# Seven block products in place of eight in a quarter of a down projection

## The chip, the cores and the metric

The kernel runs on one core of a Trainium2 chip. TensorE multiplies 128x128 blocks and writes into PSUM, VectorE (DVE) and ScalarE (ACT) compute on SBUF and PSUM, GpSimd (POOL) does a little, and SyncE (SP) issues the loads from HBM. The metric is device time in microseconds, from the runs' own clock; the profile shows one execution of the same program, instruction by instruction.

## The reference

One layer of a hybrid trunk on 256 tokens of width 2048, all in float32: a mixer (mLSTM heads, forgetting attention and a gated convolution), then a feed-forward layer, which is what the change touches.

```python
    x = x + jnp.concatenate([y_m, y_a, y_c], axis=-1) @ w_out
    h2 = rmsnorm(x, norm_ffn)
    x = x + jnp.square(jax.nn.relu(h2 @ w_up)) @ w_down
    ...
    return rmsnorm(x, final_norm)
```

`w_up` is 2048x8192 and `w_down` 8192x2048.

## The kernel before

Every large product is made in float32 precision from two rounded parts: an operand is split into a high part (`hi`, type fp32r) and the rest (`lo`), and three products hi*hi, hi*lo and lo*hi are added up in PSUM. Activations are split once; weights are split as they arrive.

The weights come as a stream of units of 1 MiB (`unit`, `load`, L304 and L326), four rows of blocks (k) by 512 columns for `w_down`, into four raw tiles in turn (`NRAW`). A unit is worked in two steps. For step i, ACT copies half a unit to a `hi` tile (L368) and DVE subtracts to get `lo` (L387); there are five tiles of each (`NHL`), so the split of step i+5 can begin only when TensorE is through with step i. When both halves are split, the raw tile is free and SP loads the unit four further on.

The feed-forward layer runs in four quarters of 2048 hidden features. In each, four up blocks (kind "B") give the hidden features transposed, which are joined (L441, L447), squared where positive (L1131) and split into `hid` (L1135, L1137). Then four down blocks (kind "A") of 512 output columns follow one after the other, each over all 16 k of the quarter; a step is 12 matmuls of 512 columns, two k by two halves of the tokens (j) by three products, into two PSUM banks (`mm` and `mx` have four banks each and alternate by block). A finished bank is scaled and added to the residual `x2t` by DVE (L1149).

The order on each engine is not written by hand. A list schedule (`issue`, `best`, `run`, L131 to L171) keeps an estimated clock for each engine, and always issues the task that can start by that clock with the lowest `prio`. The result is a fixed order on each engine, in which the chip then runs the instructions, each with its semaphore waits. DVE's additions to the residual have prio -2, the splits -1, and the two lines that make them are

```python
        a = t_act(ca(1024), hi, deps, prio=prio)
        b = t_dve(cd(1024), lo, [a], prio=prio)
```

Of the kernel before, what the change touches and what calls it, by code (L numbers as in the profile page):

```python
# [33 lines left out]
def trunk(ctx: ExitStack, tc, x, norm_mix, w_in, b_in, mlstm_conv_w, mlstm_conv_b,  # L34
# [24 lines left out]
    # ---- emission: a list schedule on estimated engine clocks  # L59
# [6 lines left out]
    class Buf:  # L66
        """One tile of a rotation of n: taken when the tile n before it has no readers left."""
# [40 lines left out]
    def room(takes):  # L108
        """When the buffers are free; None while a reader of the old tile is not yet issued."""
# [84 lines left out]
    # ---- pools  # L194
# [21 lines left out]
    # ---- loads of x, parameter rows  # L216
# [33 lines left out]
    # x lies where the values and the attention operands come later  # L250
# [6 lines left out]
    # ---- constants  # L257
# [30 lines left out]
    def small(n=2):  # L288
        """Columns of the tile of statistics."""
# [6 lines left out]
    # ---- weight stream  # L296
# [11 lines left out]
    def unit(b, src, c0, k0, last, gates=0, gside=None):  # L308
        """One MiB of weights: columns c0.. of src (and the gate columns beside them)."""
        n = 4 if b.w == 512 else 8  # L310
        units.append(dict(b=b, src=src, c0=c0, ks=list(range(k0, k0 + n)), w=b.w,
                          g=gates, gside=gside, last=last, first=not b.started))
# [43 lines left out]

    def split_tasks(i, deps):
        """High and low parts of half a unit."""
        u, h = divmod(i, 2)
        if u >= len(units):  # L360
            return
        d = units[u]
# [9 lines left out]
        a = t_act(ca(1024), hi, deps, prio=prio)  # L372
# [23 lines left out]

    def matmuls(i, toks):
        u, half = divmod(i, 2)
# [56 lines left out]
    # ---- parameter columns  # L455
# [11 lines left out]
    # the array's clock rises once it is kept busy: transposes of the identity while x arrives  # L467
# [9 lines left out]
    # ---- x: norm, transpose, split  # L477
# [61 lines left out]
    # ---- late constants and parameters  # L539
# [57 lines left out]
    # ---- values  # L597
# [27 lines left out]
    # ---- conformer branch  # L625
# [101 lines left out]
    # ---- the other values, forgetting attention's operands  # L727
# [17 lines left out]
    # ---- gates  # L745
# [14 lines left out]
    def build_gates():  # L760
# [12 lines left out]
        # log1p(e) = ln(u) + (e - (u - 1)) / u with u = fl(1 + e)  # L773
# [503 lines left out]
```

## Time and profile before

| what | us |
|---|---|
| median of 3 runs (1150.33, 1153.60, 1153.37) | 1153.37 |
| the profiled execution, by its span (the page shows no other time of it) | 1148.2 |
| TensorE busy in it | 1133.9 |
| DVE busy | 717.3 |
| ACT busy | 574.3 |

The span runs from the first to the last instruction, so the time of a run is some 5 us longer (1153.37 - 1148.2 = 5.2). Busy time of TensorE counts pipelined matmuls, each from its start to its modelled end, so that one engine can be "99% busy" with matmuls that overlap; what one matmul costs is read from the chain of waits, as a length divided by a count.

### The profile page before, as it was taken

The page shows a single profiled execution, that of the slowest core. Times are in us where ns is not written, and L with a number is a line of the kernel's source. Part 1 is how long each engine was busy: PE and PEld are TensorE (multiplying, and loading weights), DVE is VectorE, ACT ScalarE, POOL GpSimd, SP SyncE. Part 2 cuts the span into 40 slices and gives each one's busy share as a digit, 9 for nine tenths or more (in the row PEclk, how much of TensorE's full clock was granted, in tenths as well). Part 3 has the DMA queues.
Part 4 walks back from the last instruction along what each step waited for, and adds up shares of the span by engine and source line. Part 5 has one row for each costly group of instructions (what it writes and reads, how often), then busy time and mean ns, then how long its engine had stood idle before and what let it go on. Part 6 is the DMA issues. An engine that isn't in the chain of part 4 may idle for free.

```text
span 1148.2 us, 14812 instructions
## 1 busy us (share of the span) xinstructions
PE 1133.9 (99%) x5880; PEld 965.3 (84%) x5880; DVE 717.3 (62%) x978; ACT 574.3 (50%) x807; POOL 17.6 (2%) x40
## 2 busy tenths in 40 slices
PE   8999999999999999999999999999999999999996
PEld 7888888888888888888888888888888888888885
DVE  6679988886665556556545655544655554566553
ACT  6455366777864545444344444333544333454442
POOL 1000000000000000000000000000000000000000
PEclk9999999999999999999999999999999999999999
DMA  8756654557546556655566655566655566655542
GB/s 304 242 184 191 199 164 148 151 153 248 169 162 220 184 185 184 190 199 196 184 189 193 189 193 190 184 191 195 189 193 187 184 192 199 190 189 184 183 147 74
DMA packets 127692, 214.91 MB, mean 187 GB/s; under 512 B 3676, under 2 KB 44936, under 8 KB 127240
## 3 DMA queue, kind: packets, MB, share of 16 engines
q1 hardware_dynamic: 127016, 212.92, 57.9%
q8 instruction: 46, 0.75, 0.3%
q10 hardware_dynamic: 608, 1.06, 0.3%
q14 instruction: 22, 0.18, 0.0%
HBM read 211.87 MB, written 2.10 MB: 186 GB/s over the span
## 4 chain that ended last, share of the span: by engine, by line
PE 97%; DMA 1%; issue 0%; ACT 0%; DVE 0%; SPq 0%; POOL 0%; POOLq 0%; ACTq 0%; DVEq 0%
PE mm L57 64%; PE mx L57 32%; DMA x<-in_x_dram 1%; PE mx L1085 0%; SPq L255 0%; PE mx L846 0%; POOL st L294 0%; PE mx L531 0%; ACT x2t L1188 0%; PE mx L879 0%; DVE lo L387 0%; ACT junk L1175 0%; POOLq L1272 0%; ACT hi L368 0%; PE mx L705 0%
## 5 line engine op out<-in xcount | busy, mean ns | idle before, releaser
L387 DVE TENSOR_TENSOR lo<-raw,hi 128x1024 fp32r<-128x1024 f32 x392 | 480.1, 1225 | 384.8 <-ACT hi L368 383.4
L368 ACT ACTIVATE hi<-raw 128x1024 fp32r<-128x1024 f32 x392 | 415.5, 1061 | 507.4 <-PE mm L57 317.8
L57 PE MATMUL mm<-x,hi 128*128 128x512 f32 x640 | 227.8, 400 | 0.0
L57 PE MATMUL mm<-h,hi 128*128 128x512 f32 x512 | 180.7, 397 | 0.0
L57 PE MATMUL mx<-h,hi 128*128 128x512 f32 x512 | 180.4, 397 | 0.0
L57 PE MATMUL mm<-x,lo 128*128 128x256 f32 x640 | 179.4, 280 | 0.0
L57 PE MATMUL mm<-hi,hid 128*128 128x512 f32 x512 | 159.0, 389 | 0.0
L57 PE MATMUL mx<-hi,hid 128*128 128x512 f32 x512 | 158.9, 389 | 0.0
L57 PEld LDWEIGHTS mm<-x,hi 128*128 128x128 f32 x640 | 120.2, 188 | 28.9 <-ACT tmp L443 0.4
L57 PE MATMUL mm<-h,lo 128*128 128x256 f32 x512 | 143.7, 281 | 0.0
L57 PE MATMUL mx<-h,lo 128*128 128x256 f32 x512 | 143.7, 281 | 0.0
L57 PEld LDWEIGHTS mm<-x,lo 128*128 128x128 f32 x640 | 120.9, 189 | 0.1
L57 PEld LDWEIGHTS mm<-h,hi 128*128 128x128 f32 x512 | 96.1, 188 | 23.3 <-DVE x2t L1073 0.2
L57 PEld LDWEIGHTS mx<-h,hi 128*128 128x128 f32 x512 | 96.1, 188 | 23.3
L57 PEld LDWEIGHTS mm<-hi,hid 128*128 128x128 f32 x512 | 96.1, 188 | 20.1
L57 PEld LDWEIGHTS mx<-hi,hid 128*128 128x128 f32 x512 | 96.1, 188 | 20.0
L57 PE MATMUL mm<-lo,hid 128*128 128x512 f32 x256 | 99.6, 389 | 0.0
L57 PE MATMUL mx<-lo,hid 128*128 128x512 f32 x256 | 99.6, 389 | 0.0
L57 PEld LDWEIGHTS mm<-h,lo 128*128 128x128 f32 x512 | 96.7, 189 | 0.2
L57 PEld LDWEIGHTS mx<-h,lo 128*128 128x128 f32 x512 | 96.7, 189 | 0.0
L57 PE MATMUL mm<-hi,y 128*128 128x512 f32 x256 | 80.4, 392 | 0.0
L57 PE MATMUL mm<-hi,x 128*128 128x512 f32 x192 | 61.6, 396 | 0.0
(191 smaller groups left out, 872.6 us busy)
## 6 DMA issues: line engine op xcount, KB each, us to landing
raw<-in_w_up_dram SPq DMA_DIRECT2D x64, 1024.0 KB, 5.3
raw<-in_w_down_dram SPq DMA_DIRECT2D x64, 1024.0 KB, 5.2
raw<-in_w_in_dram SPq DMA_DIRECT2D x45, 1024.0 KB, 5.3
raw<-in_w_out_dram SPq DMA_DIRECT2D x16, 1024.0 KB, 5.3
raw<-in_w_in_dram SPq DMA_DIRECT2D x4, 1032.0 KB, 5.1
raw<-in_w_in_dram SPq DMA_DIRECT2D x2, 1088.0 KB
x<-in_x_dram SPq DMA_DIRECT2D x8, 256.0 KB, 6.0
x2t<-in_x_dram SPq DMA_DIRECT2D x2, 1024.0 KB
```

The costliest lines, as they stand in the source:

```text
L57: pe.matmul(o, l, r, start=start, stop=stop, skip_group_check=True)
L368: act.activation(t, raws[u][0][:, h * n:(h + 1) * n, :], AF.Copy)
L387: dve.tensor_sub(hl[i][1], raws[u][0][:, h * n:(h + 1) * n, :], hl[i][0].bitcast(F32))
```

## The change

In each quarter the down blocks are taken in pairs (columns 0 to 1023 and 1024 to 2047), and for the second of the four groups of four k (`SV = 1`) the pair's product is made by a method of Strassen's kind: the activations of the group are a 2x2 arrangement of blocks (two k by two halves of the tokens), the weights another (two k by two blocks of 512 columns), and the product takes seven block products of 6 matmuls where it took eight. This is done for seven of the eight pairs; the last pair of the last quarter is left as it was.

For that, the group's activations are summed four ways and split (`x_sums`, once a quarter), and the weights are summed in place in the raw tiles by DVE, four sums a pair (`sum_task`), between the splits. The products run in the order p3, p1, p2, p5, p7, p6, p4 (`SEVEN`). Three go straight into banks of the pair. Four (p1, p5, p6, p7) go into banks of their own, and since the seven products of all quarters are combined in the same way, these four are only accumulated in SBUF (`add_up`): in the first quarter ACT copies them there, in the later ones DVE adds them. In the last quarter that a pair takes part in (quarter 4 for the first pair, 3 for the second) DVE combines the four sums and adds them to the residual: four additions and four scaled additions of 512 columns, with prio -1.5. The load of the last gain (`fnb`, 1 MiB), whose tile now also holds a pair's sums, moves from before the feed-forward layer to the end of that.

```diff
-    def unit(b, src, c0, k0, last, gates=0, gside=None):
-        """One MiB of weights: columns c0.. of src (and the gate columns beside them)."""
+    def unit(b, src, c0, k0, last, gates=0, gside=None, seven=None):
...
+    steps = []
+    sums = {}
+    SEVEN = (("p3", 0, 1), ("p1", 1, 0), ("p2", 1, 1), ("p5", 1, 0), ("p7", 0, 0), ("p6", 0, 1), ("p4", 1, 1))
+    def make_steps():
+        for u, d in enumerate(units):
+            if d["seven"] is None:
+                steps.extend(dict(u=u, h=h, p=None) for h in range(2))
+            elif d["seven"][0]:
+                steps.extend(dict(u=u - 1 + x, h=h, p=p, o=d["seven"][1], e=u) for p, x, h in SEVEN)
+    def piece(u, h):
+        return raws[u][0][:, 2 * h:2 * h + 2, :]
+    def sum_task(i):
+        s = steps[i]
+        e, p = s["e"], s["p"]
+        o, l, r = {"p5": ((e, 0), (e - 1, 0), (e, 0)),
+                   "p7": ((e - 1, 0), (e - 1, 1), (e - 1, 0)),
+                   "p6": ((e - 1, 1), (e - 1, 1), (e, 0)),
+                   "p4": ((e, 1), (e, 1), (e - 1, 1))}[p]
+        after = [halves[i - {"p5": 2, "p7": 3, "p6": 5, "p4": 4}[p]]] + [sums[k] for k in (i - 1, i - 2) if k in sums]
+        sums[i] = t_dve(cd(1024), lambda: dve.tensor_sub(piece(*o), piece(*l), piece(*r)),
+                        after + [loaded[e - 1], loaded[e]], prio=-1)
+        return sums[i]
+    def split_seven(i, deps):
+        s = steps[i]
+        u, h = s["u"], s["h"]
+        if s["p"] in ("p5", "p7", "p6", "p4"):
+            deps = deps + [sum_task(i)]
+        def hi():
+            t = sbt(base, [P, 2, 512], "hi", F32R, bufs=NHL)
+            hl[i] = [t, sbt(base, [P, 2, 512], "lo", F32R, bufs=NHL)]
+            act.activation(t, piece(u, h), AF.Copy)
+        a = his[i] = t_act(ca(1024), hi, deps + [loaded.setdefault(u, Task("none", 0.0, None)), his[i - 1]], prio=-1)
+        halves[i] = t_dve(cd(1024), lambda: dve.tensor_sub(hl[i][1], piece(u, h), hl[i][0].bitcast(F32)),
+                          [a], prio=-1)
+        if s["p"] == "p4":
+            e = s["e"]
+            f1 = [sums[i], halves[i - 1], halves[i - 2]]
+            f2 = [halves[i], halves[i - 3]]
+            c = t_ctl(lambda: load(e - 1 + NRAW, max(t.fin for t in f1)), f1)
+            t_ctl(lambda: load(e + NRAW, max(t.fin for t in f2)), f2 + [c])
+    his = {}
...
+        a = his[i] = t_act(ca(1024), hi, deps + [his.get(i - 1)], prio=prio)
...
+    def seven_matmuls(i):
+        s = steps[i]
+        o, p = s["o"], s["p"]
+        stat = o["hid"]()
+        hi, lo = hl[i]
+        ks = units[s["u"]]["ks"]
+        plain = {"p1": (0, 0), "p2": (2, 0), "p4": (2, 1)}
+        ps = {"p2": lambda: o["b"][0].bufs[0].t, "p3": lambda: o["b"][1].bufs[0].t,
+              "p4": lambda: o["b"][0].bufs[1].t}.get(p, lambda: o["extra"][p].t)()
+        own = p not in ("p2", "p3", "p4")
+        for ii in range(2):
+            if p in plain:
+                m, j = plain[p]
+                k = ks[m + ii] % KC
+                xh = stat[:, k, j * P:(j + 1) * P]
+                xl = stat[:, k, S + j * P:S + (j + 1) * P]
+            else:
+                m = {"p5": 0, "p6": 1, "p7": 2, "p3": 3}[p]
+                xh, xl = (o["sums"]()[:, v_, m, ii, :] for v_ in range(2))
+            mul(ps, xh, hi[:, ii, :], own and ii == 0, False)
+            mul(ps, xh, lo[:, ii, :], False, False)
+            mul(ps, xl, hi[:, ii, :], False, own and ii == 1)
...
-        x2["fn"] = sbt(pl("late"), [P, D], "fnb")
-        nc.sync.dma_start(x2["fn"], bcast(final_norm, D))
...
+    SV = 1
+    xsum, acc = {}, {}
+    def x_sums(q, wb, d, prev):
+        def f1():
+            t = xsum["f"] = sbt(pl("late"), [P, 4, 2, P], "xsum")
+            b11, b21, b12, b22 = (wb.t[:, 2 * k:2 * k + 2, j * P:(j + 1) * P] for k in range(2) for j in range(2))
+            dve.tensor_add(t[:, 0], b21, b22)
+            dve.tensor_sub(t[:, 1], t[:, 0], b11)
+            dve.tensor_sub(t[:, 2], b11, b21)
+            dve.tensor_sub(t[:, 3], b12, t[:, 1])
+        def f2():
+            xsum["s"] = sbt(pl("late"), [P, 2, 4, 2, P], "xsums", F32R)
+            act.activation(xsum["s"][:, 0], xsum["f"], AF.Copy)
+        d = t_dve(4 * cd(256), f1, [d] + prev, prio=-1.85, uses=[wb])
+        a = t_act(ca(1024), f2, [d] + prev, prio=-1.85)
+        return t_dve(cd(1024), lambda: dve.tensor_sub(xsum["s"][:, 1], xsum["f"], xsum["s"][:, 0].bitcast(F32)),
+                     [a], prio=-1.85)
+    def fn_in():
+        x2["fn"] = sbt(pl("late"), [P, D], "fnb")
+        nc.sync.dma_start(x2["fn"], bcast(final_norm, D))
+    def add_up(p, q, o, fin):
+        ts = []
+        for m, x in enumerate(("p1", "p5", "p6", "p7")):
+            def f(m=m, x=x):
+                if (p, 0) not in acc:
+                    acc[p, 0] = sbt(pl("late"), [P, 4, 512], "acc0") if p == 0 else \
+                        sbt(pl("late"), [P, D], "fnb").rearrange("p (m n) -> p m n", m=4)
+                t = acc[p, 0][:, m, :]
+                if q == 0:
+                    act.activation(t, o["extra"][x].t, AF.Copy)
+                else:
+                    dve.tensor_add(t, t, o["extra"][x].t)
+            deps = [o["done"][x], late_open] + ts[-1:]
+            if q == 0:
+                ts.append(t_act(ca(512, True), f, deps, prio=-2, uses=[o["extra"][x]]))
+            else:
+                ts.append(t_dve(cd(512), f, deps, prio=-2, uses=[o["extra"][x]]))
+        if not fin:
+            return []
+        def g(i):
+            a1, a5, a6, a7 = (acc[p, 0][:, m, :] for m in range(4))
+            def out(j, c, t):
+                dve.scalar_tensor_tensor(x2[0][:, j, cut(c)], t, rs2[:, j:j + 1], x2[0][:, j, cut(c)],
+                                         op0=OP.mult, op1=OP.add)
+            if i == 0:
+                dve.tensor_add(a6, a6, a1)
+                out(0, 2 * p, a1)
+            elif i == 1:
+                dve.tensor_add(a7, a7, a6)
+                out(1, 2 * p, a7)
+            elif i == 2:
+                dve.tensor_add(a6, a6, a5)
+                out(0, 2 * p + 1, a6)
+            else:
+                dve.tensor_add(a5, a5, a7)
+                out(1, 2 * p + 1, a5)
+        gs = [ts[-1]]
+        for i in range(4):
+            gs.append(t_dve(2 * cd(512), lambda i=i: g(i), [gs[-1], rs_t], prio=-1.5))
+        return gs[1:]
...
+        t0, t1 = (("mm", "mx"), ("mx", "mm"))[q % 2]
         for c in range(4):
-            b = block_units(blk("B", 512, lambda: big["h"], "h", tag()), w_up, 2048 * q + 512 * c)
+            b = block_units(blk("B", 512, lambda: big["h"], "h", (t0, t1)[c % 2]), w_up, 2048 * q + 512 * c)
...
+            if c == SV:
+                chunk["sums%d" % q] = x_sums(q, wb, done_zz, prev)
         hid_readers = []
+        def down(c, tg):
+            return blk("A", 512, lambda: big["hid"], "hid%d" % q, tg)
+        bs, shared = {}, {}
+        for p in range(2):
+            if q == 3 and p == 1:
+                for c in (2, 3):
+                    bs[c] = block_units(down(c, t1), w_down, 512 * c, KC * q)
+                continue
+            b0, b1 = bs[2 * p], bs[2 * p + 1] = down(2 * p, t0), down(2 * p + 1, t0)
+            names = ("p1", "p5", "p6", "p7")
+            o = dict(b=(b0, b1), tag=t1, hid=lambda: big["hid"], sums=lambda: xsum["s"], q=q,
+                     extra={x: Buf(mx_rot if t1 == "mx" else mm_rot) for x in names},
+                     done={x: Task("pe", 0.0, None) for x in names})
+            for g in range(4):
+                k0 = KC * q + 4 * g
+                if g == SV:
+                    unit(b1, w_down, 1024 * p + 512, k0, False, seven=(0, o))
+                    unit(b0, w_down, 1024 * p, k0, False, seven=(1, o))
+                else:
+                    unit(b0, w_down, 1024 * p, k0, g == 3)
+                    unit(b1, w_down, 1024 * p + 512, k0, g == 3)
+            got = add_up(p, q, o, q == (3, 2)[p])
+            for i, t in enumerate(got):
+                shared[2 * p + i // 2, i % 2] = t
+            if p == 1 and got:
+                fn_t = t_ctl(fn_in, got)
         for c in range(4):
-            b = block_units(blk("A", 512, lambda: big["hid"], "hid%d" % q, tag()), w_down, 512 * c, KC * q)
+            b = bs[c]
...
+            p, o = steps[i]["p"], steps[i]["o"]
+            new = [o["extra"][p]] if p in o["extra"] else []
+            need = [halves[i], chunk["sums%d" % o["q"]]] + [chunk[d["b"].key, k % KC] for k in d["ks"]]
+            force(lambda: all(t.fin is not None for t in need) and room(new) is not None)
+            start = max([clock["pe"], room(new)] + [t.fin + LAT for t in need])
+            take(new)
+            for x_ in new:
+                x_.t = bank(o["tag"])
+            seven_matmuls(i)
+            clock["pe"] = start + 1.3
+            if new:
+                o["done"][p].fin = clock["pe"]
+            split_tasks(i + NHL, [done_at(clock["pe"])])
+            extras()
+            continue
```

The first place where the order matters is DVE in the second quarter, where the down products begin. Before, its rows are these (`lo` is a weight split, `zz` and `hid` the hidden features, `x2t` the residual):

```order
L447 TENSOR_TENSOR z<-tmp,mx 128x256 x4
L1131 SCALAR_TENSOR_TENSOR zz<-z 128x1024
L387 TENSOR_TENSOR lo<-raw,hi 128x1024 x2
L1137 TENSOR_TENSOR hid<-zz,hid 128x4x256
L387 TENSOR_TENSOR lo<-raw,hi 128x1024 x6
L1149 SCALAR_TENSOR_TENSOR x2t<-mm,st,x2t 128x512 x2
L387 TENSOR_TENSOR lo<-raw,hi 128x1024 x8
L1149 SCALAR_TENSOR_TENSOR x2t<-mx,st,x2t 128x512 x2
```

With the change, DVE's rows there, from the split of the fourth product on (line numbers are those of the changed kernel; L383 sums raw weights, L399 splits the weights of a product, L1218 adds a product in the bank `mm` to `acc0`, L443 splits the weights of ordinary steps, and a bracket names the engines whose semaphores a row waits for):

```order
L399 TENSOR_TENSOR lo_6250<-raw_6096,hi_6249 128x1024 [waits Activation_49]
L399 TENSOR_TENSOR lo_6260<-raw_6057,hi_6259 128x1024 [waits Activation_49]
L1218 TENSOR_TENSOR acc0_4918<-acc0_4918,mm_6262 128x512 [waits PE_49]
L399 TENSOR_TENSOR lo_6271<-raw_6057,hi_6270 128x1024 [waits Activation_49]
L1218 TENSOR_TENSOR acc0_4918<-acc0_4918,mm_6280 128x512 [waits PE_49]
L383 TENSOR_TENSOR raw_6096<-raw_6096,raw_6057 128x1024
L1218 TENSOR_TENSOR acc0_4918<-acc0_4918,mm_6298 128x512 [waits PE_49]
L1218 TENSOR_TENSOR acc0_4918<-acc0_4918,mm_6289 128x512
L399 TENSOR_TENSOR lo_6306<-raw_6096,hi_6305 128x1024 [waits Activation_49]
L443 TENSOR_TENSOR lo_6313<-raw_6138,hi_6312 128x1024 [waits DMAHW7_49,Activation_49]
```

Between the splits there now stand the additions of p1, p5, p6 and p7, in this order, each after a product of TensorE. The split of the seventh product (`lo_6306`, of p4) comes behind the last two of them. The same order stands in quarters 3 and 4 for the first pair.

In the fourth quarter the first pair's sums are also combined. DVE's rows from the sum for p4 on:

```order
L383 TENSOR_TENSOR raw_8826<-raw_8826,raw_8787 128x1024
L1218 TENSOR_TENSOR acc0_4918<-acc0_4918,mm_9028 128x512 [waits PE_49]
L1218 TENSOR_TENSOR acc0_4918<-acc0_4918,mm_9019 128x512
L1236 TENSOR_TENSOR acc0_4918<-acc0_4918 128x512 [waits DVE_49]
L1232 SCALAR_TENSOR_TENSOR x2t_2582<-acc0_4918,st_99,x2t_2582 128x512
L1239 TENSOR_TENSOR acc0_4918<-acc0_4918 128x512 [waits DVE_49]
L1232 SCALAR_TENSOR_TENSOR x2t_2582<-acc0_4918,st_99,x2t_2582 128x512 [waits DVE_49]
L1242 TENSOR_TENSOR acc0_4918<-acc0_4918 128x512
L1232 SCALAR_TENSOR_TENSOR x2t_2582<-acc0_4918,st_99,x2t_2582 128x512 [waits DVE_49]
L1245 TENSOR_TENSOR acc0_4918<-acc0_4918 128x512
L1232 SCALAR_TENSOR_TENSOR x2t_2582<-acc0_4918,st_99,x2t_2582 128x512 [waits DVE_49]
L399 TENSOR_TENSOR lo_9036<-raw_8826,hi_9035 128x1024 [waits Activation_49]
```

The eight rows of L1236 to L1245 and L1232 moved in ahead of the seventh product's split (`lo_9036`).

The third place is DVE for the second pair of the third quarter, where that pair's sums are combined; the rows from the split of the first ordinary step on (`lo_7952`):

```order
L443 TENSOR_TENSOR lo_7952<-raw_7813,hi_7951 128x1024 [waits DMAHW7_49,Activation_49]
L1218 TENSOR_TENSOR fnb_5218<-fnb_5218,mx_7968 128x512 [waits PE_49]
L1218 TENSOR_TENSOR fnb_5218<-fnb_5218,mx_7954 128x512
L1236 TENSOR_TENSOR fnb_5218<-fnb_5218 128x512 [waits DVE_49]
L1232 SCALAR_TENSOR_TENSOR x2t_2582<-fnb_5218,st_99,x2t_2582 128x512
L1239 TENSOR_TENSOR fnb_5218<-fnb_5218 128x512 [waits DVE_49]
L1232 SCALAR_TENSOR_TENSOR x2t_2582<-fnb_5218,st_99,x2t_2582 128x512 [waits DVE_49]
L1242 TENSOR_TENSOR fnb_5218<-fnb_5218 128x512
L1232 SCALAR_TENSOR_TENSOR x2t_2582<-fnb_5218,st_99,x2t_2582 128x512 [waits DVE_49]
L1245 TENSOR_TENSOR fnb_5218<-fnb_5218 128x512
L1232 SCALAR_TENSOR_TENSOR x2t_2582<-fnb_5218,st_99,x2t_2582 128x512 [waits DVE_49]
L443 TENSOR_TENSOR lo_7965<-raw_7813,hi_7964 128x1024 [waits Activation_49]
```

Here the seventh product's split is already ahead, and what stands behind the additions and the combination is the split of the second ordinary step (`lo_7965`).

## Rows read from the trace of the kernel before

**Rows 1.** The page: the span, the engines' busy times, and TensorE's granted clock by 40 slices

```profile
span 1148.2 us, 14812 instructions
PE 1133.9 (99%) x5880; PEld 965.3 (84%) x5880; DVE 717.3 (62%) x978; ACT 574.3 (50%) x807; POOL 17.6 (2%) x40
...
PEclk9999999999999999999999999999999999999999
```

**Rows 2.** The chain of waits in order of time: start, length, engine and line of two blocks

```profile
1029.38 22.61 PE mx L57 x128
...
1073.77 21.76 PE mx L57 x96
```

**Rows 3.** Busy time of the engines in the down products of the third quarter

```profile
874.48:961.54 87.06, 87.06 (x385) 72.07 (x385) 46.70 (x44) 35.21 (x35) 0.00 (x0) 1.00 0.59 193
```

**Rows 4.** Groups of instructions by line, the whole span

```profile
L387 DVE TENSOR_TENSOR lo<-raw,hi 128x1024 fp32r<-128x1024 f32 x392 | 480.1, 1225 | 384.8 <-ACT hi L368 383.4
L368 ACT ACTIVATE hi<-raw 128x1024 fp32r<-128x1024 f32 x392 | 415.5, 1061 | 507.4 <-PE mm L57 317.8 <-PE mx L57 182.5 <-issue 2.9
...
L664 DVE SCALAR_TENSOR_TENSOR cacc<-ypad,colp,cacc 128x256 f32<-128x256 f32 x120 | 51.7, 479 | 0.0
...
L1131 DVE SCALAR_TENSOR_TENSOR zz<-z 128x1024 f32<-128x1024 f32 x16 | 19.6, 1225 | 0.5
...
L1149 DVE SCALAR_TENSOR_TENSOR x2t<-mm,st,x2t 128x512 f32<-128x512 f32 x16 | 11.2, 745 | 0.0
...
L1073 DVE TENSOR_TENSOR x2t<-x2t,mm 128x512 f32<-128x512 f32 x8 | 5.1, 680 | 0.0
L1066 ACT ACTIVATE junk<-x2t 128x512 bf16<-128x512 f32 x8 | 5.0, 622 | 0.1
...
L1157 DVE TENSOR_TENSOR x2t<-x2t,fnb 128x512 f32<-128x512 f32 x6 | 3.9, 686 | 0.0
```

**Rows 5.** The timeline where the first down product begins, ACT and DVE

```profile
519.77 1.05 ACT L368 ACTIVATE hi<-raw 128x1024 fp32r<-128x1024 f32 x1
520.36 1.23 DVE L1131 SCALAR_TENSOR_TENSOR zz<-z 128x1024 f32<-128x1024 f32 x1
522.25 1.06 ACT L368 ACTIVATE hi<-raw 128x1024 fp32r<-128x1024 f32 x1 [1.43 <-PE mm L57]
523.22 1.04 ACT L1135 ACTIVATE hid<-zz 128x1024 fp32r<-128x1024 f32 x1
```

**Rows 6.** The timeline 11 us later, at a step's end

```profile
529.98 0.62 PE L57 MATMUL mm<-hi,hid 128*128 128x512 f32 x2
530.41 1.06 ACT L368 ACTIVATE hi<-raw 128x1024 fp32r<-128x1024 f32 x1 [1.66 <-PE mm L57]
...
531.50 1.23 DVE L387 TENSOR_TENSOR lo<-raw,hi 128x1024 fp32r<-128x1024 f32 x1 [1.49 <-ACT hi L368]
```

**Rows 7.** Issues of the weight loads: size and time to landing

```profile
raw<-in_w_down_dram SPq DMA_DIRECT2D x64, 1024.0 KB, 5.2
```

**Rows 8.** The timeline of TensorE near the start of the span

```profile
8.56 0.23 PE L461 MATMUL mx<-ident,rowp 16*128 16x16 f32 x1
12.38 3.36 PE L531 MATMUL mx<-ident,x 128*128 128x128 f32 x16 [3.60 <-DVE x L511]
```

**Rows 9.** Busy time and granted clock by stretches, start and end of the span

```profile
10.00:12.00 2.00, 0.00 (x0) 0.00 (x0) 1.10 (x5) 1.90 (x4) 0.01 (x1) 1.00 1.05 407
12.00:14.00 2.00, 1.61 (x9) 1.62 (x10) 1.93 (x5) 1.17 (x3) 2.00 (x5) 0.69 1.06 402
14.00:16.00 2.00, 2.00 (x10) 1.63 (x8) 1.10 (x2) 2.00 (x5) 0.01 (x1) 0.50 1.04 382
16.00:18.00 2.00, 1.86 (x7) 1.14 (x7) 2.00 (x4) 2.00 (x4) 0.00 (x0) 0.96 1.06 389
...
1139.00:1140.00 1.00, 0.05 (x1) 0.00 (x0) 0.88 (x2) 0.40 (x2) 0.00 (x0) 1.00 1.05 346
...
1142.00:1143.00 1.00, 0.00 (x0) 0.00 (x0) 0.88 (x2) 0.72 (x1) 0.00 (x0) 0.78 0.00 0
```

More of the change, by code (lines that the diff above doesn't have):

```diff
@@ L306, in __init__ @@
             self.need = {}
-    def unit(b, src, c0, k0, last, gates=0, gside=None):
+    def unit(b, src, c0, k0, last, gates=0, gside=None, seven=None):
         n = 4 if b.w == 512 else 8
         units.append(dict(b=b, src=src, c0=c0, ks=list(range(k0, k0 + n)), w=b.w,
-                          g=gates, gside=gside, last=last, first=not b.started))
+                          g=gates, gside=gside, last=last, first=not b.started, seven=seven))
         b.started = True
@@ L357, in split_tasks @@
+    his = {}
     def split_tasks(i, deps):
-        u, h = divmod(i, 2)
-        if u >= len(units):
+        if i >= len(steps):
             return
+        if steps[i]["p"]:
+            split_seven(i, deps)
+            return
+        u, h = steps[i]["u"], steps[i]["h"]
         d = units[u]
@@ L371, in split_tasks @@
         prio = -1 if i >= NHL else -2.005 + 0.02 * i
-        a = t_act(ca(1024), hi, deps, prio=prio)
+        a = his[i] = t_act(ca(1024), hi, deps + [his.get(i - 1)], prio=prio)
         last = [a]
@@ L395, in split_tasks @@
             t_ctl(lambda: load(u + NRAW, max(t.fin for t in frees)), frees)
+    def seven_matmuls(i):
[20 more added lines that the diff above has]
+            mul(ps, xl, hi[:, ii, :], False, own and ii == 1)
     def matmuls(i, toks):
-        u, half = divmod(i, 2)
+        u, half = steps[i]["u"], steps[i]["h"]
         d = units[u]
@@ L1102, in trunk @@
     z_rot, zz_rot = Rot(2), Rot(2)
-    flip = [0]
-    def tag():
-        flip[0] ^= 1
-        return ("mx", "mm")[flip[0]]
+    SV = 1
[15 more added lines that the diff above has]
+                     [a], prio=-1.85)
@@ L1114, in trunk @@
     for q in range(4):
-        down_of = []
+        t0, t1 = (("mm", "mx"), ("mx", "mm"))[q % 2]
         for c in range(4):
-            b = block_units(blk("B", 512, lambda: big["h"], "h", tag()), w_up, 2048 * q + 512 * c)
+            b = block_units(blk("B", 512, lambda: big["h"], "h", (t0, t1)[c % 2]), w_up, 2048 * q + 512 * c)
             zb, wb = Buf(z_rot), Buf(zz_rot)
@@ L1131, in f1 @@
                 dve.scalar_tensor_tensor(wb.t, zb.t, 0.0, zb.t, op0=OP.max, op1=OP.mult)
-            d = t_dve(cd(1024), f1, js[1:], prio=-1.9, takes=[wb], uses=[zb])
+            d = done_zz = t_dve(cd(1024), f1, js[1:], prio=-1.9, takes=[wb], uses=[zb])
             prev = hid_readers if q else []
@@ L1154, in trunk @@
                         junk[:, 0:512], x2[0][:, j, cut(c)], AF.Square, scale=D ** -0.5,
-                        accum_out=ss3[:, 4 * j + c:4 * j + c + 1]), [d], prio=-2)
+                        accum_out=ss3[:, 4 * j + c:4 * j + c + 1]), [d, shared.get((c, j))], prio=-2)
                     fsq[j].append(a)
                     fin_t[j].append(t_dve(cd(512), lambda j=j, c=c: dve.tensor_mul(
-                        x2[0][:, j, cut(c)], x2[0][:, j, cut(c)], x2["fn"][:, cut(c)]), [a], prio=-1))
+                        x2[0][:, j, cut(c)], x2[0][:, j, cut(c)], x2["fn"][:, cut(c)]), [a, fn_t], prio=-1))
+    make_steps()
     last = units[-1]["b"]
@@ L1197, in trunk @@
     NU = len(units)
-    items = [(i, (0, 1)) for i in range(2 * NU - 4)]
+    NS = len(steps)
+    items = [(i, (0, 1)) for i in range(NS - 4)]
     for j in range(2):
-        items += [(i, (j,)) for i in range(2 * NU - 4, 2 * NU)]
+        items += [(i, (j,)) for i in range(NS - 4, NS)]
     dma[0] = 7.9
@@ L1208, in trunk @@
     for i, toks in items:
-        u, half = divmod(i, 2)
+        u, half = steps[i]["u"], steps[i]["h"]
         d = units[u]
+        if steps[i]["p"]:
+            p, o = steps[i]["p"], steps[i]["o"]
[13 more added lines that the diff above has]
+            continue
         b = d["b"]
```

## The prediction, made before the changed kernel was run

> **What bounds the kernel now.** Read the page first: TensorE is busy for 1133.9 of 1148.2 us, DVE for 717.3, ACT for 574.3, and the granted clock is at full speed in all 40 slices [rows 1]. Busy time could mislead, so the chain of waits comes next: in the feed-forward layer it is TensorE alone, block after block, an up block 22.61 us and a down block 21.76 us for 96 matmuls [rows 2]. One matmul of the down product thus costs 21.76 / 96 = 0.227 us, an ordinary step of 12 costs 2.72, one of 6 costs 1.36. Nothing in that chain is a wait. So a matmul less is time gained, as long as its operands come in time; the rest of this text is about whether they do. In the timeline ACT's copy starts some 0.2 us after the next step has begun (530.21 is the second start in the first row), having sat idle 1.66 us for TensorE; DVE's split follows at once after 1.49 us idle [rows 6]. In the down product DVE is busy 46.70 of 87.06 us [rows 3]. The cover is there, but it is 1.5 us a step and not one long stretch.
>
> **What the change removes.** Six matmuls in each of 7 pairs: 42 x 0.227 = 9.5 us, all on the path. [...]
>
> **What it adds, by pair.** Three more copies at 1.061 us on ACT; on DVE three more splits and four sums in place, seven at 1.225 (the split has the same shape), and from the second quarter on four additions from PSUM at 0.68 [rows 4]. That is 8.6 + 2.7 = 11.3 us of DVE for a pair, 22.6 in a quarter. With the 46.7 of [rows 3] it makes 69.3 us of 84.3, so as an average DVE still has room. The sums of the activations (four additions of 256 columns, at most 0.479 each, and one copy and split, 3.2 us of DVE) lie in the up product a whole block ahead of their use, beside idle time; I cost them at nothing. The load of the gain goes between two weight loads, behind DVE's last combination; the load queued behind it needs a later split on DVE anyway, lands 5.2 us after its issue [rows 7] and is read seven steps (19 us) later: nothing. Up to the first of these sums the order of all engines is that of before, but for the gain's load. PSUM: a pair takes the four banks of one kind, and a bank is emptied by 0.745 us of DVE while another block's two steps (5.4 us) run: nothing.
>
> **Where the order bites.** Count from the first matmul of the seven products; they end at 1.36, 2.72, ... and the seventh (p4) should start at 8.16 and wants its `lo` for its second matmul, at 8.39. A result can be read 0.2 us after its grid time.
>
> *First pair, quarters 2, 3 and 4.* DVE's order has the addition of p6 ahead of the split for p4. p6 is the sixth product, ready at 8.16 + 0.2 = 8.36, after which come two additions (1.36) and the split (1.225): 10.95, and 11.0 at TensorE with a hand-over of 0.05. TensorE wanted it at 8.39, so it stands 2.6 us. It doesn't win this back, since it is the bound. The next split is ready 1.2 us later, when the seventh product still runs and the next one wants it 1.36 us on: no second stall. In quarter 4 the combination stands ahead of that split too: four additions at 0.686 [rows 4] and four scaled additions. For the latter no row has 512 columns from SBUF; between 0.479 (256 columns) and 1.225 (1024) a straight line gives 0.73. Together 5.7, so 2.6 + 5.7 = 8.3 us.
>
> *Second pair, quarter 3.* The seventh split is in time, and so is the first ordinary one (done at 8.8). Behind it: two additions to 10.1, the combination to 15.8, then the second ordinary split, 17.0. TensorE wants that at 12.24 + 0.23 = 12.47: 4.6 us.
>
> *Quarter 1.* ACT does the copying, and the copy for the seventh product stands behind that of p5, which is ready at 5.64: 5.64 + 0.62 + 1.06 + 1.225 = 8.6: 0.2 us late for the first pair; for the second pair everything is in time, as it is in quarter 2 (p5's addition done at 6.3, the seventh split at 7.5).
>
> Stalls: 0.2 + 2.6 + 2.6 + 8.3 + 4.6 = 18.3 us. Against 9.5 saved: 8.8 us longer.
>
> **Does a waiting instruction hold those behind it?** That carries the sum. The trace shows it on ACT: `zz` was done at 521.59, yet the copy of `hid` from it waited until 523.22, behind a copy of weights for which ACT sat idle 1.43 us [rows 5]. No row shows it of DVE, where it could be worth anything from nothing to 18 us; I take it to be as on ACT, which is built into the program in the same way. [...]
>
> **The clock.** Near the start TensorE stood 3.6 us [rows 8]. [...] The stalls of 8.3 and 4.6 us are longer than the gap at the start, those of 2.6 shorter. I charge the two long ones half of 3.4 us each, 3.4 together, bounded below by nothing and above by 6.8 (all four).
>
> **Sum.** 1148.2 - 9.5 + 18.3 + 3.4 = 1160.4 us of span. The median of the runs is 5.2 us above this execution's span, which lies outside it: 1165.6 us, 1.1% slower. Bounds: without a clock effect 1162; with it at all four stalls 1169; scaled additions at 0.48 instead of 0.73 take 2 us off, at 1.225 they would add 4.
>
> **Rivals.**
> *The additions don't hold the splits* (DVE passes over a waiting addition, or finds p6 ready). Decisive point: the split for p4 done by 8.39. Then all is hidden but 0.2 us, and the time is 1153.4 - 9.5 + 0.2 = 1144, faster. For it: the averages of [rows 3], 15 us of idle DVE in a quarter even after the change. Against: the rows of the order, and ACT's held copy. Chance 0.07.
> *Only the waits hold, not the combinations*: if the eight combination rows took far less time or TensorE ran on during them, the stalls would be 0.2 + 3 x 2.6 = 8.0, with no long gap for the clock: 1153.4 - 9.5 + 8.0 = 1151.9, no change. Against: the additions of 512 columns have a row. Chance 0.07.
> *DVE becomes the bound after the stalls.* In the 9.5 us of a seven-product run it has 11 x 1.225 + 2.7 = 16.2 us of work; if the lead of five steps is used up before, each of the next steps waits as well, 1 to 2 us a pair, and the clock falls more often: above 1171. For it: that figure. Against: in the up product and the first four steps it has 1.5 us free a step [rows 6]. Chance 0.1.
>
> **How the numbers follow.** The forecast has 0.76 and its own range is 1159 to 1171. To hold 8 in 10 the range reaches a little toward the second rival: 1157 to 1171. A measurement of this kernel can tell about 0.3% (3.5 us) from no change: faster below 1149.9, slower above 1156.8. The forecast, the third rival and a sliver of the second are slower: 0.87; no change 0.06; faster 0.07.
>
> **What would show it.** TensorE: 5838 matmuls in place of 5880; a gap of some 2.6 us before the second matmul of the seventh product in the first pair of quarters 2 and 3, 8 us in quarter 4, 4.6 us in the second pair of quarter 3 before the second ordinary step, each with DVE's split as the releaser; DVE idle 0.8 us before the addition of p6. A granted clock of 0.5 after the two longest. Right but for the clock: gaps as said and full clock. Wrong: no gap above 1 us in the down products, or gaps at every step.

## The result, and the profile after

The changed kernel takes **1166.3 us** (median of 4 runs, 1164.51 to 1167.03) against 1152.01 for the kernel before (4 runs, 1150.33 to 1153.6): a ratio of 1.0123, 95% interval 1.0106 to 1.0141. It is slower by 1.2%; the prediction was 1165.6.

The page of the changed kernel, with the span and the engines as in [rows 1]; the profiled execution took 1167.01 us. Of the clock's 40 slices the first and the 38th show 8 tenths, where all showed 9 before:

```profile
span 1164.9 us, 14898 instructions
PE 1135.5 (97%) x5838; PEld 962.3 (83%) x5838; DVE 804.3 (69%) x1083; ACT 602.3 (52%) x840; POOL 17.6 (2%) x40
```

The 42 matmuls are gone (5838 for 5880), yet TensorE shows 1.6 us more busy time: a matmul at half clock is shown longer (0.63 us for 0.39), and the up blocks of quarter one took longer too (last section). What TensorE waited for, over the whole span (total, times, longest):

```profile
PE mx L57 <- DVE lo L399: 8.7, 2, 7.1
PE mm L57 <- DVE lo L443: 3.8, 1, 3.8
...
PE mm L57 <- DVE lo L399: 1.6, 1, 1.6
...
PE mx L57 <- ACT hi L396: 0.7, 2, 0.4
PE mm L57 <- ACT hi L396: 0.4, 1, 0.4
```

L399 is the split of the low part for the seven products, L443 that for ordinary steps, L396 the copy of the high part for the seven products; `...` stands for waits at the start of the span. The seven waits lie in four places: 0.4 for `hi` and then 1.6 for `lo` in the first pair of quarters two and three, 3.8 in quarter three's second pair, 0.4 and 7.1 in quarter four. All are waits for DVE's split or for the copy ahead of it, where [rows 2] had none. The longest, in the timeline of DVE and then of TensorE:

```profile
1078.59 1.28 DVE L1218 TENSOR_TENSOR acc<-acc,mm 128x512 f32<-128x512 f32 x2 [0.90 <-PE mm L57]
1079.79 0.69 DVE L1236 TENSOR_TENSOR acc<-acc 128x512 f32<-128x512 f32 x1
...
1084.55 0.75 DVE L1232 SCALAR_TENSOR_TENSOR x2t<-acc,st,x2t 128x512 f32<-128x512 f32 x1
1085.22 1.22 DVE L399 TENSOR_TENSOR lo<-raw,hi 128x1024 fp32r<-128x1024 f32 x1
```

```profile
1078.92 0.50 PE L57 MATMUL mx<-hi,hid 128*128 128x512 f32 x1 [0.37 <-ACT hi L396]
1086.50 0.79 PE L57 MATMUL mx<-lo,hid 128*128 128x512 f32 x1 [7.07 <-DVE lo L399]
```

DVE stands idle 0.90 us for the sixth product, adds two products, does the eight rows of the combination, and only then the split that TensorE has wanted since 1079.15, one matmul start after 1078.92.

The down products of the four quarters, the last to the end of the span: length, then the busy time of PE, PEld, DVE, ACT and POOL, the granted clock, DMA's share and GB/s. Before, they were 87.06 [rows 3], and 1148.2 - 1051.99 = 96.2 for the last [rows 1, 2]:

```profile
522.45:607.04 84.59, 84.59 (x373) 69.75 (x373) 62.31 (x58) 44.77 (x49) 0.00 (x0) 1.00 0.58 199
697.48:786.00 88.52, 86.51 (x373) 70.89 (x373) 66.93 (x66) 40.99 (x41) 0.00 (x0) 0.98 0.55 190
876.44:969.04 92.60, 86.79 (x373) 70.87 (x373) 72.15 (x74) 41.01 (x41) 0.00 (x0) 0.98 0.56 193
1059.49:1164.90 105.41, 88.71 (x378) 72.29 (x377) 66.13 (x80) 42.74 (x58) 1.87 (x2) 0.93 0.38 130
```

Quarter one gains 2.5 us; the others lose 1.5, 5.5 and 9.2. That is +13.7 of the +16.7 us between the two spans; the other 3.0 lie outside the change (last section). The granted clock by short stretches, after the waits of quarters two, three (second pair) and four:

```profile
720.00:723.00 3.00, 3.00 (x8) 2.32 (x7) 3.00 (x4) 1.71 (x2) 0.00 (x0) 0.50 0.95 309
...
948.00:952.00 4.00, 3.67 (x9) 2.96 (x10) 4.00 (x5) 0.00 (x0) 0.00 (x0) 0.57 0.85 317
...
1082.00:1091.00 9.00, 4.50 (x11) 3.54 (x12) 8.93 (x11) 1.72 (x2) 0.00 (x0) 0.50 0.37 132
```

With the slices beside them these are 3.4, 3.4 and 10.2 us at half clock (granted 0.50). There a matmul starts 0.42 us after the one ahead (949.78 and 950.20) in place of 0.227, so by these two starts about half of such a stretch is lost, as far as TensorE works in it.

### The profile page after: what moved, and what is told of

It reads as the page before. It is cut to its first block, busy times and chain, and to the rows that moved or that the text cites. A ratio compares the mean times of both kernels' runs of the same rounds, so it can differ in the third digit from the quotient of the medians.

```text
span 1164.9 us, 14898 instructions
## 1 busy us (share of the span) xinstructions
PE 1135.5 (97%) x5838; PEld 962.3 (83%) x5838; DVE 804.3 (69%) x1083; ACT 602.3 (52%) x840; POOL 17.6 (2%) x40
## 3 DMA queue, kind: packets, MB, share of 16 engines
q10 hardware_dynamic: 608, 1.06, 0.3%
## 4 chain that ended last, share of the span: by engine, by line
PE 95%; DVE 2%; DMA 1%; issue 1%; ACT 0%; POOL 0%; POOLq 0%; ACTq 0%; DVEq 0%
PE mm L57 65%; PE mx L57 29%; DMA x<-in_x_dram 1%; DVE lo L399 0%; DVE x2t L1232 0%; DVE lo L443 0%; PE mx L1162 0%; DMA rowp<-in_norm_mix_dram 0%; DVE acc L1218 0%; PE mx L925 0%; POOL st L294 0%; PE mx L610 0%; ACT x2t L1362 0%; PE mx L958 0%; DVE fnb L1218 0%
## 5 line engine op out<-in xcount | busy, mean ns | idle before, releaser
L443 DVE TENSOR_TENSOR lo<-raw,hi 128x1024 fp32r<-128x1024 f32 x364 | 442.5, 1224 | 288.4 <-ACT hi L424 287.0
L424 ACT ACTIVATE hi<-raw 128x1024 fp32r<-128x1024 f32 x364 | 384.2, 1061 | 426.9 <-PE mm L57 282.1
L57 PE MATMUL mm<-x,hi 128*128 128x512 f32 x640 | 227.8, 400 | 0.0
L57 PE MATMUL mm<-h,hi 128*128 128x512 f32 x512 | 181.5, 399 | 0.0
L57 PE MATMUL mx<-h,hi 128*128 128x512 f32 x512 | 181.2, 399 | 0.0
L57 PE MATMUL mm<-x,lo 128*128 128x256 f32 x640 | 179.5, 280 | 0.0
L57 PE MATMUL mm<-hi,hid 128*128 128x512 f32 x556 | 174.6, 391 | 0.4 <-ACT hi L396 0.4
L57 PEld LDWEIGHTS mm<-x,hi 128*128 128x128 f32 x640 | 120.2, 188 | 28.8 <-ACT tmp L522 0.4
L57 PE MATMUL mm<-h,lo 128*128 128x256 f32 x512 | 143.8, 281 | 0.0
L57 PE MATMUL mx<-h,lo 128*128 128x256 f32 x512 | 143.8, 281 | 0.0
L57 PEld LDWEIGHTS mm<-hi,hid 128*128 128x128 f32 x556 | 105.2, 189 | 22.7 <-ACT hi L396 0.8
L57 PEld LDWEIGHTS mm<-x,lo 128*128 128x128 f32 x640 | 120.9, 189 | 0.1
L57 PEld LDWEIGHTS mm<-h,hi 128*128 128x128 f32 x512 | 96.2, 188 | 24.0 <-DVE x2t L1150 0.2
L57 PEld LDWEIGHTS mx<-h,hi 128*128 128x128 f32 x512 | 96.2, 188 | 23.9
L57 PE MATMUL mm<-lo,hid 128*128 128x512 f32 x278 | 109.3, 393 | 5.4 <-DVE lo L443 3.8
L57 PE MATMUL mx<-hi,hid 128*128 128x512 f32 x328 | 106.0, 399 | 0.7 <-ACT hi L396 0.7
L57 PEld LDWEIGHTS mm<-h,lo 128*128 128x128 f32 x512 | 96.7, 189 | 0.1
L57 PEld LDWEIGHTS mx<-h,lo 128*128 128x128 f32 x512 | 96.7, 189 | 0.1
L396 ACT ACTIVATE hi<-raw 128x1024 fp32r<-128x1024 f32 x49 | 52.1, 1064 | 66.2 <-DVE raw L383 27.0
L57 PE MATMUL mm<-hi,y 128*128 128x512 f32 x256 | 80.4, 392 | 0.0
L57 PEld LDWEIGHTS mx<-hi,hid 128*128 128x128 f32 x328 | 63.4, 193 | 15.2 <-ACT hi L396 1.6
L57 PE MATMUL mx<-lo,hid 128*128 128x512 f32 x164 | 65.8, 401 | 8.7 <-DVE lo L399 8.7
```

What stands on the lines that cost most here:

```text
L57: pe.matmul(o, l, r, start=start, stop=stop, skip_group_check=True)
L396: act.activation(t, piece(u, h), AF.Copy)
L424: act.activation(t, raws[u][0][:, h * n:(h + 1) * n, :], AF.Copy)
L443: dve.tensor_sub(hl[i][1], raws[u][0][:, h * n:(h + 1) * n, :], hl[i][0].bitcast(F32))
```

## The experiments

The theory under test: what costs is work that stands ahead of a split in DVE's order, plus the clock behind each wait, and not the amount of DVE's work. Its rivals: DVE has too much to do in whatever order, or the clock falls for reasons of its own.

### The splits first

Three priorities of the program's list schedule, so that a split which is ready goes ahead:

```diff
-                ts.append(t_act(ca(512, True), f, deps, prio=-2, uses=[o["extra"][x]]))
+                ts.append(t_act(ca(512, True), f, deps, prio=-0.9, uses=[o["extra"][x]]))
...
-                ts.append(t_dve(cd(512), f, deps, prio=-2, uses=[o["extra"][x]]))
+                ts.append(t_dve(cd(512), f, deps, prio=-0.9, uses=[o["extra"][x]]))
...
-            gs.append(t_dve(2 * cd(512), lambda i=i: g(i), [gs[-1], rs_t], prio=-1.5))
+            gs.append(t_dve(2 * cd(512), lambda i=i: g(i), [gs[-1], rs_t], prio=-0.8))
```

> The changed kernel, with the accumulations (lines 1222 and 1224) and the combinations (line 1250) given a later priority than the splits; every instruction stays, the matmuls too, so the saved 42 x 0.227 = 9.5 us stay as well. Only two additions of a pair, of its first and fourth products, can still stand ahead of the seventh product's split.
> Theory (what costs is work that stands ahead of a split on DVE, in order, and the clock that falls behind it): the waits for lo L399 (8.7 + 1.6 us) and for lo L443 (3.8 us) go, and so do the stretches at half clock behind them (about 7 us, from the quarters' lengths: 2.5 in each of three). 1166.3 - 14 - 7 = about 1145, range 1141 to 1149, ratio to before 0.991 to 0.997, with the granted clock at 1.00 through all four down quarters.
> Rival 1 (DVE has too much to do in the eleven steps of a group, in whatever order): the waits come back at later splits or at the next up block, 1158 or more.
> Rival 2 (the clock falls for a reason of its own, not behind waits): the waits go and the half clock stays, about 1152.

Measured: **1142.57 us** (5 runs, 1141.25 to 1144.2), ratio to before **0.9921** (0.9909 to 0.9933). The page (span 1142.1 us), all that TensorE still waited for, DVE's timeline at the place in quarter two where the changed kernel had its wait, and the four down products:

```profile
PE 1128.1 (99%) x5838; PEld 958.7 (84%) x5838; DVE 803.9 (70%) x1083; ACT 601.3 (53%) x840; POOL 17.6 (2%) x40
```

```profile
PE mx L610 <- DVE x L590: 3.0, 1, 3.0
PE mm L550 <- POOL gb L272: 1.4, 1, 1.4
PE mm L57 <- ACT x L594: 0.2, 1, 0.2
```

```profile
712.42 1.22 DVE L383 TENSOR_TENSOR raw<-raw 128x1024 f32<-128x1024 f32 x1
713.55 1.28 DVE L1218 TENSOR_TENSOR acc<-acc,mm 128x512 f32<-128x512 f32 x2
714.84 1.22 DVE L399 TENSOR_TENSOR lo<-raw,hi 128x1024 fp32r<-128x1024 f32 x1
715.99 5.76 DVE L443 TENSOR_TENSOR lo<-raw,hi 128x1024 fp32r<-128x1024 f32 x5
721.90 1.23 DVE L443 TENSOR_TENSOR lo<-raw,hi 128x1024 fp32r<-128x1024 f32 x1 [0.15 <-ACT hi L424]
723.04 0.68 DVE L1218 TENSOR_TENSOR acc<-acc,mm 128x512 f32<-128x512 f32 x1
```

```profile
522.56:607.17 84.61, 84.61 (x374) 69.76 (x373) 62.23 (x58) 44.70 (x49) 0.00 (x0) 1.00 0.58 199
697.62:781.96 84.34, 84.34 (x373) 69.84 (x373) 66.92 (x66) 40.94 (x41) 0.00 (x0) 1.00 0.58 200
872.40:956.75 84.35, 84.35 (x374) 69.85 (x373) 72.16 (x74) 40.95 (x41) 0.00 (x0) 1.00 0.60 205
1047.19:1142.10 94.91, 85.70 (x378) 70.62 (x377) 65.77 (x80) 42.68 (x58) 1.87 (x2) 0.97 0.42 144
```

The same instructions in another order, with the same DVE work in quarter two (66.92 and 66.93 us), and every wait behind the span's start is gone, and in the down products the half clock too (1.00 in the first three; the 0.97 of the last goes to the end of the span, and up to 1127.0 it is 1.00 as well). Both rivals fall. Only two additions, of the first and the fourth product, still stand ahead of the seventh split, and DVE waits for neither; the third comes only after six ordinary splits, when DVE has idle time again, and the fourth after one more. Quarters two and three are now 87.06 - 84.35 = 2.7 us shorter than before, which is the twelve matmuls saved in a quarter at 0.227. This version beats both kernels.

### The combinations alone held back

```diff
-            gs.append(t_dve(2 * cd(512), lambda i=i: g(i), [gs[-1], rs_t], prio=-1.5))
+            gs.append(t_dve(2 * cd(512), lambda i=i: g(i), [gs[-1], rs_t, o["done"]["sum"]], prio=-1.5))
...
+    def release(i):
+        for i7, o in after_seven:
+            for x in o["late"]:
+                if i == i7 + o["late"][x]:
+                    o["done"][x].fin = clock["pe"]
...
```

> The changed kernel, with the combinations alone (line 1250) held until five ordinary steps behind the seventh product; the four accumulations of a pair stay where they are.
> Theory (each piece of work ahead of a split is charged by itself): the wait of the first pair in quarter four falls from 7.1 us to that of quarters two and three (1.6 us for lo L399), the wait of quarter three's second pair (3.8 us) goes; three equal waits of some 2 us in all are left. 1166.3 - 5.5 - 3.8 = 1157.0 by the waits alone, and up to 5 us less if the clock no longer falls at those two places: 1152 to 1157, most likely 1154, ratio 1.002 to 1.005.
> Rival (the accumulations alone hold the split, the combination is taken up by slack behind it): no change, about 1166.

Measured: 1150.52 us (12 runs), ratio 0.9998 (0.9989 to 1.0007). The down products of quarters two to four:

```profile
695.83:782.75 86.92, 84.90 (x373) 69.75 (x373) 66.85 (x66) 40.92 (x41) 0.00 (x0) 1.00 0.58 194
873.19:960.12 86.93, 84.91 (x374) 69.75 (x373) 69.91 (x72) 40.94 (x41) 0.00 (x0) 1.00 0.54 184
1050.56:1148.00 97.44, 86.26 (x378) 70.53 (x377) 65.60 (x80) 42.68 (x58) 1.87 (x2) 0.98 0.41 140
```

Against the splits-first version each is longer by 2.58, 2.58 and 2.53 us. That is the price of a pair's accumulations where the changed kernel has them, without a combination and the same in three places. That it comes out level with before was not expected: my range began at 1152, because I left some of the half clock in place, and here it fell at none of the three waits (1.00 from 714 to 724, 891 to 901 and 1069 to 1079 us). The rival (1166) is far off: against the first profile of the changed kernel quarter three is 5.7 us shorter and quarter four 8.0, which is what the combinations cost there, with their waits and what the clock took behind them.

### A ladder of waits

Accumulations and combinations held back, and the seventh split written several times:

```diff
-        halves[i] = t_dve(cd(1024), lambda: dve.tensor_sub(hl[i][1], piece(u, h), hl[i][0].bitcast(F32)),
+        halves[i] = t_dve(cd(1024), lambda: [dve.tensor_sub(hl[i][1], piece(u, h), hl[i][0].bitcast(F32)) for _ in range(1 + (s["o"]["again"] if s["p"] == "p4" else 0))],
...
+            o = dict(again=(2, 3, 3, 5, 4, 4, 1)[2 * q + p], b=(b0, b1), tag=t1, hid=lambda: big["hid"], sums=lambda: xsum["s"], q=q,
...
```

> The changed kernel with accumulations and combinations held until two to five steps behind the seventh product, so that none stands ahead of a split, and with the seventh product's split (line 399) written again 2, 3, 3, 5, 4, 4 and 1 times in the seven pairs in their order (each 1.22 us on DVE, the same values again). This makes seven waits of TensorE of seven sizes: by the recurrence of the steps about 2.2, 1.6, 3.4, 4.0, 4.7, 2.8 and 1.0 us.
> Theory 1 (the clock falls behind a wait above some size): waits up to 1.6 us leave the clock at 1.00, those from 2.8 us on are each followed by a stretch at 0.50, and each costs the time of a stall plus about 2 to 2.5 us; 19.7 us of waits, 8 to 13 us of clock, so a span of about 1170 to 1178.
> Theory 2 (whether the clock falls does not go by the wait's size): some of the waits from 2.8 us on leave the clock at 1.00, or one below 1.7 us drops it.

One run, 1167.58 us with a span of 1165.5. The seven waits in TensorE's timeline, in order:

```profile
540.61 0.50 PE L57 MATMUL mm<-lo,hid 128*128 128x512 f32 x1 [1.73 <-DVE lo L399]
...
584.49 0.50 PE L57 MATMUL mm<-lo,hid 128*128 128x512 f32 x1 [1.43 <-DVE lo L399]
...
720.44 0.79 PE L57 MATMUL mx<-lo,hid 128*128 128x512 f32 x1 [2.99 <-DVE lo L399]
...
769.63 0.50 PE L57 MATMUL mx<-lo,hid 128*128 128x512 f32 x1 [3.94 <-DVE lo L399]
...
908.40 0.79 PE L57 MATMUL mm<-lo,hid 128*128 128x512 f32 x1 [4.25 <-DVE lo L399]
...
956.25 0.50 PE L57 MATMUL mm<-lo,hid 128*128 128x512 f32 x1 [2.69 <-DVE lo L399]
...
1089.64 0.50 PE L57 MATMUL mx<-lo,hid 128*128 128x512 f32 x1 [0.47 <-DVE lo L399]
```

In the first pairs one, two, three and four extra splits give 0.47, 1.73, 2.99 and 4.25 us: 1.26 more for each; in the second pairs three, four and five give 1.43, 2.69 and 3.94. Once the slack is gone, one instruction more ahead of the split costs TensorE the time by which DVE starts the next row later. That is 1.26 us here, where the copies write the same tile (five of them span 6.26 us from 902.09 on); the five splits of different tiles in the splits-first version span 5.76, which is 1.14 for each. This is the order's effect measured by itself, with no wait of DVE for TensorE in it. The clock behind the third, fourth, fifth and sixth of them:

```profile
720.00:726.00 6.00, 5.56 (x13) 4.40 (x14) 6.00 (x6) 1.06 (x1) 0.00 (x0) 0.50 0.74 254
...
771.00:774.00 3.00, 3.00 (x9) 2.35 (x8) 3.00 (x3) 1.06 (x1) 0.00 (x0) 0.50 0.92 335
...
908.00:914.00 6.00, 5.60 (x13) 4.44 (x14) 6.00 (x6) 1.06 (x1) 0.00 (x0) 0.50 0.75 241
...
952.00:962.00 10.00, 7.31 (x32) 5.74 (x32) 9.90 (x10) 4.25 (x4) 0.00 (x0) 1.00 0.69 231
```

With the slices beside them, 6.8 us at half clock at the wait of 2.99 and again at that of 4.25, but 3.4 at that of 3.94 and none at that of 2.69: what the clock takes does not grow with the wait. In this one run it fell behind the three longest waits and none of the shorter ones, as theory 1 has it; against theory 1 stands the first profile of the changed kernel, where it fell behind a wait of 1.64. The span came out below the 1170 to 1178 that were expected: by the lengths of the down products the waits cost about 19 us (19.7 expected) and the clock 7.6 (8 to 13), and the rest of this execution is 3.0 us shorter than in the splits-first profile (its first down product starts at 519.57, there at 522.56).

### The changed kernel twice more

> The changed kernel once more, unchanged, for a second profile. In its first profile the equal waits of quarters two and three (0.38 and 1.64 us) left the clock at 1.00 in one place and dropped it in the other, and the waits of 3.8 and 7.1 us dropped it both times.
> Theory (which waits drop the clock does not go by their size alone, and differs between executions): the waits stand at the same places with the same sizes to 0.1 us, the stretches at half clock at others or of other lengths; the span moves by 1 to 3 us with them.
> Rival (the program fixes it): the same three stretches, after the first wait of quarter two, after quarter three's second pair and in quarter four, and the up blocks of quarter one at 22.61 us again.

> The same once more, a third profile of the changed kernel: if the stretches at half clock are fixed by the program, all three profiles agree in their places and lengths; if not, at least one of the three differs, most likely at one of the two short waits (0.4 and 1.6 us) of the first pairs of quarters two and three.

1162.49 and 1166.05 us, spans 1160.3 and 1164.0, both on another chip than the experiments above. The seven waits stand in the same places and agree to 0.01 us in all three profiles. The clock does not. The second profile is 4.6 us shorter than the first, more than the 1 to 3 that were expected, but 3.1 of that lie ahead of the first down product. Its down products of quarters two to four, with full clock in quarter two:

```profile
694.40:781.31 86.91, 84.90 (x374) 69.76 (x373) 66.84 (x66) 40.93 (x41) 0.00 (x0) 1.00 0.57 194
871.75:964.39 92.64, 86.83 (x374) 70.80 (x373) 72.17 (x74) 40.92 (x41) 0.00 (x0) 0.98 0.56 193
1054.83:1160.30 105.47, 88.90 (x379) 72.44 (x377) 66.13 (x80) 42.65 (x58) 1.87 (x2) 0.93 0.39 130
```

and the third profile's clock at the four places:

```profile
718.00:721.00 3.00, 3.00 (x9) 2.35 (x8) 3.00 (x4) 1.22 (x2) 0.00 (x0) 0.50 0.96 341
...
896.00:898.00 2.00, 2.00 (x6) 1.52 (x6) 2.00 (x3) 1.14 (x2) 0.00 (x0) 0.50 0.97 242
...
947.00:953.00 6.00, 5.69 (x13) 4.46 (x14) 4.80 (x5) 0.59 (x1) 0.00 (x0) 0.50 0.80 282
...
1083.00:1089.00 6.00, 2.33 (x6) 1.87 (x7) 5.93 (x8) 0.00 (x0) 0.00 (x0) 0.50 0.12 33
```

At the first pair's wait of quarters two and three the clock fell once in the first profile, never in the second, both times in the third. So the waits are the same in all three executions, and the clock behind them differs from one to the next; the second and the third profile come from the same chip. Why it differs was not tried.

## Why the prediction was right

**The saving.** 42 matmuls at 0.227 were to give 9.5 us. The splits-first version shows them: its down products are 2.5, 2.7, 2.7 and 1.3 us shorter than before, 9.2 in all, with 0.25 in quarter one lost to the copy on ACT that was priced at 0.2 (that order on ACT is the same in the splits-first version).

**The order of DVE.** The step that carried the sum, that a waiting instruction on DVE holds those behind it, was inferred from ACT's rows. Now there are rows of DVE itself, in quarter two of the changed kernel:

```profile
713.86 0.69 DVE L1218 TENSOR_TENSOR acc<-acc,mm 128x512 f32<-128x512 f32 x1 [0.89 <-PE mm L57]
714.47 1.22 DVE L383 TENSOR_TENSOR raw<-raw 128x1024 f32<-128x1024 f32 x1
...
715.80 1.06 ACT L396 ACTIVATE hi<-raw 128x1024 fp32r<-128x1024 f32 x1 [4.63 <-DVE raw L383]
```

DVE sits idle 0.89 us for the fourth product (p5), and behind that addition stands the sum for the seventh (L383), which waits for no engine. It starts 16.99 us after the quarter's first down product (714.47 - 697.48). In the splits-first version it starts after 14.80 (712.42 - 697.62), when p5 has only begun; so it could have run, and was held. The sign that was named, DVE idle 0.8 us ahead of the sixth product's addition, came true as well (0.89 in this quarter, 0.90 in quarter four), but shows less: the split behind it got its `hi` only at 716.86 (715.80 + 1.06), after that idle time, which ended at 716.58.

The prediction left this hold out: the sum and the `hi` copy of the seventh product are nowhere on its path, and the wait of 0.4 for `hi` was not foreseen. The size came out right because the path that was foreseen ends last: the split could begin at 716.86, and the additions of p6 and p7 keep it until 717.78. By these rows about 1.6 of the 2.6 us would stay if those two additions alone were moved; that is an estimate, which no run tried.

**The stalls**, each as the length of a down product over the splits-first version's, with the half clock behind it taken off:

- First pair, quarters two and three, predicted 2.6: the second profile has 86.91 - 84.34 = 2.57, at full clock.
- Second pair, quarter three, predicted 4.6: 92.64 - 84.35 - 2.57 = 5.7, of which half of 3.4 is clock: 4.0.
- Quarter four, predicted 8.3: 105.47 - 94.91 = 10.6, of which half of the 5.6 us at half clock after the wait's end is clock: 7.8.

With 0.25 they sum to 17.2 against 18.3. The combination was mis-sized: its scaled addition takes 0.75 for the estimated 0.73, but the eight rows run from 1079.79 to 1085.22, 5.4 and not 5.7, since here a row of DVE begins a little before the one ahead has run its shown length (the two additions ahead, 1.28 us long from 1078.59, end at 1079.87).

**The clock.** This step was the weakest. I charged 3.4 us: half of 3.4 at each of the two long waits. The 3.4 is an estimate from [rows 9]: between 1.00 and 0.50, the shares of the clock from 12 to 18 us make (0.62 + 1 + 0.08) x 2 us at half clock after the gap at the start. No run shows 3.4 for the two long waits together; it was 1.7 + 2.6 = 4.3 and 1.7 + 2.8 = 4.5 in the first two profiles. In the first profile the clock took about 1.7 in quarter two (where I had charged nothing), 1.7 in quarter three and 2.6 in quarter four: 6.0, inside the bounds of 0 to 6.8. In the second it took 1.7 and 2.8, together 4.5, and in the third 7.6 by the lengths of the down products (88.55, 95.25 and 104.34 us), above the bounds. The argument by a wait's length alone failed: 2.0 us of idle time dropped the clock in some executions, 2.69 in the ladder did not.

**The sum.** The span was forecast at 1160.4; the three profiles have 1160.3, 1164.0 and 1164.9. For the last: 2.6 more of clock, 1.1 less of stalls, 3.0 outside the change. That the median lies within 0.7 us of the forecast is partly luck. I set the median 5.2 us above the span, as time outside the span, and that reading was wrong: in every run that lists both, the time is 2.0 to 2.2 us above its own span. So the execution of the kernel before with the span of 1148.2 fits its fastest run (1150.33), and the other 3 us of the 5.2 are the distance of the median from that run. The changed kernel was profiled in one of its slower executions (1167.01; the median is 1.4 above that span), and the 3.0 us that it spent outside the change made up for most of that.

**The rivals.** "The additions don't hold the splits" was given 1144, and the version whose splits are not held takes 1142.6; "only the waits hold" was given 1151.9, and with the combinations held back it is 1150.5. The mechanisms were wrong for this order, the prices nearly right. The third, DVE as the bound at every step, is excluded by the splits-first version, with its 84.35 us for 72.16 of DVE's work.

## What to carry to other kernels

An engine that is busy 70% of the time, as DVE is here (69% of the span in the changed kernel), can still cost a kernel its gain: what counted here is what stood ahead of the instruction that the bound engine wanted next, in the order of its queue. Where an edit adds work that nobody waits for soon (accumulations, combinations, writes back), give it a place behind the work that feeds the bound engine, above all where it must itself wait for that engine's newest result; here three priorities turned 1.2% lost into 0.8% gained. Price such a place by counting instructions from the last moment the operand is in time: each one behind that point costs the time by which the next one starts later (1.14 to 1.26 us here). Count what the operand is made from too: here its sum stood behind an addition as well.

## What the runs showed that was not expected

**Three microseconds outside the change.** To see whether they belong to the change, the kernel before was run once more:

> The kernel before once more, unchanged, for a second profile of it. The profile of the changed kernel was some 3 us longer than before's outside the down quarters: 1.3 us in the first 40 us and 1.7 us in the four up blocks of quarter one (22.61 against 22.19 us each).
> If these 3 us are the scatter of single executions, this profile has other values there than the first one (up blocks of quarter one near 22.6 us, or the start later by 1 us or so). If they come from the change, it repeats 22.19 us and the same start.

It took 1151.80 us, with a span of 1149.7. The last up block of quarter one in the chain, of the first profile of the changed kernel and of its second one; the kernel before run again has 22.19 as well (from 498.74 on):

```profile
499.84 22.61 PE mx L57 x128
```

```profile
497.17 22.19 PE mx L57 x128
```

So the second profile of the kernel before does not decide it, but those of the changed kernel do: one program has 22.61 us in one execution and 22.19 in another. Of eight profiles two have 22.61, the first of the changed kernel and the splits-first one; the blocks of the later quarters have 22.6 in all. Why the up blocks differ was not found, and whether the chip has a part in it is not shown: the second profile is from another chip than the experiments, and that of the first is not on record.

The start scatters too: the kernel before reaches its first down product at 520.92 us here and at 519.45 in its first profile, unchanged. In the first profiles of the two kernels this goes with the clock. The first eleven matmuls of weights (L57, from some 16.4 us on) take 2.97 us in the first profile of the kernel before, 4.20 in its second and 4.46 in the first of the changed kernel; the stretch at half clock (0.50) lies from 12.8 to 16.2 us in the first of these, mostly ahead of them, and from 13.1 to 19.9 in the third.

**The clock after equal waits.** Of nine waits of the same make (0.37 and 1.64 us: two in each of three profiles, and three with the combinations held back) three were followed by half clock and six were not; those of 3.8 and 7.1 us dropped it in all three profiles, for 3.4 to 10.2 us. So this program has a scatter of some microseconds that its order of instructions does not explain.
